# Column sums of the modulation: folded in DRAM by accumulating DMAs instead of GpSimd's partition reduction

## The chip, the cores and the metric

The kernel runs on one core of a Trainium2 chip. The metric is the device time of one execution in microseconds (us). Time before: median 2902.7 us of three runs (2900.84 to 2907.55). All data are float32 in DRAM; TensorE multiplies in a float32 form in which each operand is split in two parts, so that one product takes three matmuls.

## The reference

A two-layer backbone over 512 latent and 256 context tokens, D = 1024. Each layer is FFN, mixer (gated MLP in layer 0, attention in layer 1), FFN. Every sublayer is modulated by two conditioning vectors, `c` for the latent tokens and `c_ctx` for the context tokens:

```python
def modulation(cond, w_mod, b_mod):
    m = jax.nn.silu(cond) @ w_mod + b_mod
    return jnp.split(m[..., None, :], N_MOD, axis=-1)   # N_MOD = 9

def ffn_sublayer(x, shift, scale, gate, w_in, w_out, ln_g, ln_b):
    y = swiglu(modulate(x, shift, scale), w_in, w_out)   # x * (1 + scale) + shift
    return layer_norm(ALPHA * x + 0.5 * gate * y, ln_g, ln_b)
```

For one layer `m` has nine pieces of 1024 numbers: shift, scale and gate for each of the three sublayers. The change touches only how these pieces are summed.

## The kernel before

**Sublayers.** `body` runs six sublayers in order: FFN, gated MLP and FFN of layer 0 (called 0, 1 and 2 here), then FFN, attention and a latent-only FFN of layer 1 (3, 4, 5). In each, TensorE (PE) runs the input projection, then the output projection, half of the 1024 columns at a time. The weights come as 128x512 blocks of 256 KB by DMAs from the SP queue into six buffers `raw`; ScalarE (ACT) casts each into the high part of `w` and VectorE (DVE) subtracts for the low part (`split_later`; all calls of the helper `Pinned` have line 81). Activations go out to DRAM on GpSimd's queue (`act<-stage`) and come back on SP's (`q<-act`), to be split into `acts`.

**Ends of sublayers.** At the end of an output projection (`end.run`, `closing`) each of the six blocks of 128 rows gets its last products; then DVE adds them to the residual and takes statistics (`add_gated`: `q`, `z`, `st`; `norm_stats`: `mv`, `ve`), GpSimd takes the power -1/2 (`rs`, line 174), DVE makes the bias `nb` (line 670), ACT normalises `z`, PE transposes it (`ps<-ident,z`), and GpSimd's queue stores it (`zhat<-z`, line 1808). `rs` and `nb` are not pinned: a scheduler may place them among the other instructions, while calls through `Pinned` (SP, and `self.pool`) keep the order in which the program issues them. Every engine and queue runs its instructions in order.

**Residual adds.** In the first half of the output projections of sublayers 1, 2 and 3, DVE also applies the gain and bias of the LayerNorm to the residual (`z<-z,zraw`, `residual`). In these stretches, around 1020 to 1100, 1565 to 1645 and 2085 to 2170 us, DVE has nearly as much to do per slot as PE.

**Modulation as filler.** 16 of the 18 pieces are made while the sublayers run (`MOD_PLAN` says which in which). `fill` is called about once per slot; it runs what has become due in `pending` (`later(n, f)` runs f after n more fills), then one step of `mod_unit`. For a unit (l, i), and for each half of its 1024 columns, there is one accumulator `acc` of 128x512 for each conditioning vector: two for the units before (1,5), one for the rest. In each of eight steps DVE adds a 128x512 block of `w_mod` times a column of the condition to them (`acc<-mraw,cs,acc`). Then the 128 rows of `acc` must be added up. Before, GpSimd does it in place (`partition_all_reduce`, line 370, 56 times), and a DMA of 2 KB adds row 0 (line 371) onto the bias that a DMA has put in the DRAM tile `mod` [2, 1024].

**Use of the sums.** Units with i % 3 == 2 are gates: `load_gate` reads a row by a broadcasting DMA, 128x1024, before an output projection. Of each pair of the others (shift, scale), `mod_columns`, READ_LATER = 4 fills after both are sent, reads the rows by DMAs on SP's queue (`s<-mod`, four or two, 8x128); `finish`, 3 fills later, turns them by one small PE transpose and copies them into `modT`, which the next input projection reads.

**Start of the second part of the gated MLP (sublayer 1).** The gated half `v` is spilled to DRAM on GpSimd's queue (`v_spill<-q`), six chunks of six blocks. After the last chunk its statistics give `rs` 128x6 on GpSimd, SP loads the first pieces back (`v<-v_spill`), ACT and DVE normalise them (`vn`), and PE multiplies them with the spatial weights (`ps<-w_sT,vn`). Ahead of that, PE has two projections (`ps<-h,w`) to do.

Of the kernel before, what the change touches and what calls it, by code (L numbers as in the profile page):

```python
# [1 line left out]

# [4 lines left out]

F32 = mybir.dt.float32
F32R = mybir.dt.float32r
AF = mybir.ActivationFunctionType  # L10
ALU = mybir.AluOpType
AX = mybir.AxisListType

P = 128
D = 1024
KD = D // P
# [26 lines left out]
ZRAW_BUFS = 3  # L43

READ_LATER, TURN_LATER = 4, 7

FIRST_OPEN = [(2, 0), (3, 0), (4, 0)]
SECOND_OPEN = [(2, 1), (0, 0), (3, 1), (1, 0), (4, 1), (0, 1), (5, 0), (1, 1), (5, 1)]
# [7 lines left out]
CLOSE, CLOSE_LAT = 6, 8  # L56
# [29 lines left out]
class Backbone:  # L86
# [260 lines left out]

    def mod_unit(self, l, i):

        nc, io = self.nc, self.io  # L350
        nconds = self.nconds(l, i)
        m = self.mods[l, i] = self.dram.tile([2, D], F32, name=f"mod{l}{i}")
        for c in range(nconds):
            self.pool.dma_start(m[c : c + 1, :], io["b_mod"][l, i * D : i * D + D].unsqueeze(0))
        for half in range(2):
            accs = [self.acc() for _ in range(nconds)]
            for k in range(KD):
                raw, dve = self.next_raw(), self.dve
                for c in range(nconds):
                    cs = self.cs[:, c * KD + k : c * KD + k + 1]  # L360
                    if k:
                        dve.scalar_tensor_tensor(accs[c], raw, cs, accs[c], ALU.mult, ALU.add)
                    else:
                        dve.tensor_scalar(accs[c], raw, cs, None, ALU.mult)
                self.filler_raw()
                if k < KD - 1:
                    yield
            s = slice(half * 512, half * 512 + 512)
            for c in range(nconds):
                nc.gpsimd.partition_all_reduce(accs[c], accs[c], P, bass_isa.ReduceOp.add)  # L370
                nc.gpsimd.dma_start(m[c : c + 1, s], accs[c][0:1, :], accum_op=ALU.add)
            yield
        self.mod_sent.add((l, i))
        if i % 3 == 2:
            self.mod_done.add((l, i))
        elif {(l, i - i % 3), (l, i - i % 3 + 1)} <= self.mod_sent:
            self.later(READ_LATER, lambda: self.mod_columns(l, i - i % 3))

    def nconds(self, l, i):
        return 2 if (l, i) < (1, 5) else 1  # L380
# [1 line left out]
    def mod_columns(self, l, i):  # L382

        n = self.nconds(l, i)
        srcs = [self.mods[l, x][c : c + 1, :] for c in range(n) for x in (i, i + 1)]
        view = self.modT[l][:, 0:n, i * KD : (i + 2) * KD]
        f = self.columns(view, [s.rearrange("o d -> (o d)") for s in srcs])
        assert TURN_LATER > READ_LATER

        def finish():  # L390
            f()
            self.mod_done.update({(l, i), (l, i + 1)})

        self.later(TURN_LATER - READ_LATER, finish)
# [101 lines left out]
    def load_gate(self, l, i, nblocks):  # L496
        self.need((l, i))
        gate = self.main.tile([P, 2, D], F32, tag="gate", bufs=1, name="gate")
        for c in range(2 if nblocks > NB_LAT else 1):
            self.sp.dma_start(gate[:, c], self.mods[l, i][c : c + 1, :].to_broadcast([P, D]))  # L500
        self.gate = gate

    def mod_vectors(self, l, i, nconds, prev):
# [269 lines left out]
    def out_proj_latent(self, acts, l, i, factor, end, prev):  # L773

        n = acts.n
        order = acts.orders(n, KEPT_LAT, READ_BACK_LAT)[0]
        acts.feed(0, 4)
        self.new_z(NB_LAT)
        residual = iter(())
        banks = {}  # L780
        for x in range(n - CLOSE_LAT):
            ws = self.weights(2)
            for b in range(NB_LAT):
                for half in range(2):
                    if not x:
                        banks[b, half] = self.bank()
                    self.products(banks[b, half], b, [acts.of(order[x])], ws[half : half + 1], x == 0, False)
                if b % 2:
                    self.flush()
                    self.pump(1)  # L790
                    if b == 1:
                        acts.prepare(0, x + AHEAD + 1)
                        next(residual, None)
            self.release(2)
            acts.feed(0, 4)
            if x == 1:
                residual = self.residual(prev, NB_LAT)
                next(residual, None)
                self.load_gate(l, i + 2, NB_LAT)
        for _ in residual:  # L800
            pass
        st = self.stats(NB_LAT)
        end.begin(NB_LAT)
        x = n - CLOSE_LAT + AHEAD + 1
        ws = self.weights(CLOSE_LAT)
        rest = order[n - CLOSE_LAT :]
        for b in range(NB_LAT):
            for k in range(0, CLOSE_LAT, 2):
                fs = rest[k : k + 2]
                self.products(banks[b, 0], b, [acts.of(f) for f in fs], ws[k : k + 2], False, k == CLOSE_LAT - 2)  # L810
                if not b:
                    acts.feed(0, 4)
                    for _ in range(2):
                        acts.prepare(0, x)
                        x += 1
                self.flush()
                if b == NB_LAT - 1:
                    self.release(2)
                    self.pump(2)
            self.add_gated(b, 0, banks[b, 0], factor, st[b])  # L820
        self.flush()
        ws = self.weights(CLOSE_LAT)
        self.flush()
        self.pin(False)

        def closing(b):
            self.products(banks[b, 1], b, [acts.of(f) for f in rest], ws, False)
            return [lambda: self.add_gated(b, 1, banks[b, 1], factor, st[b])], st[b]

        end.last(NB_LAT, closing)  # L830
# [1058 lines left out]
```

## Time and profile before

| | |
|---|---|
| median of three runs | 2902.7 us |
| profiled execution | 2903.88 us, span 2902.0 us |
| TensorE busy / mean granted clock | 2801.8 us (97%) / 0.990 |
| VectorE / ScalarE / GpSimd busy | 2112.4 / 1164.8 / 411.0 us |
| partition reductions on GpSimd | 56, 199.0 us in all |
| DMA bytes | 426.84 MB |

A row of the timeline gives start, duration, engine, line, operation, output and inputs, the count of merged instructions, and in brackets the idle time before it with the instruction that ended it. PE is busy nearly all the time, so what matters are the few waits on it, and its clock behind them.

### The profile page before, as it was taken

What the parts mean: (1) busy time and instruction counts of PE and PEld (TensorE: products, weight loads), DVE (VectorE), ACT (ScalarE), POOL (GpSimd) and SP (SyncE); (2) the same over time, 40 slices, a digit from 0 to 9 for tenths busy, and PEclk for the clock granted to TensorE, in tenths of its full rate; (3) what the DMA queues carried; (4) which work ended last, traced back from release to release, by engine and by line L of the source; (5) the groups of instructions that cost most, each with busy time, mean ns of one, the idle gap of its engine ahead of it and who ended that gap; (6) DMA issues with size and microseconds to landing.
All of it is one profiled execution on the core that took longest, in us unless ns stands there. A gap on an engine that the chain in (4) does not pass through costs nothing.

```text
span 2902.0 us, 40507 instructions
## 1 busy us (share of the span) xinstructions
PE 2801.8 (97%) x14454; PEld 2514.5 (87%) x14454; DVE 2112.4 (73%) x3692; ACT 1164.8 (40%) x2232; POOL 411.0 (14%) x379
## 2 busy tenths in 40 slices
PE   7899999999999999999999999999999989999998
PEld 5899988788899977899999788999978778888886
DVE  6888877587777777498787968877785577733445
ACT  6333432532344432453333226333432556632322
POOL 1010112234401112000010210000021121100001
PEclk9999999999999999999999999999999999999999
DMA  7434375355544474344335644433474423444352
GB/s 236 123 115 127 105 241 175 121 197 182 179 153 155 145 243 143 116 148 127 120 119 198 194 127 132 142 117 118 143 242 146 132 83 51 141 141 137 102 167 98
DMA packets 407090, 426.84 MB, mean 147 GB/s; under 512 B 27944, under 2 KB 308584, under 8 KB 406888
## 3 DMA queue, kind: packets, MB, share of 16 engines
q1 hardware_dynamic: 387400, 361.36, 40.4%
q0 software_dynamic: 19488, 62.90, 6.8%
q8 instruction: 113, 1.85, 0.3%
q14 instruction: 89, 0.73, 0.1%
HBM read 362.95 MB, written 63.41 MB: 147 GB/s over the span
## 4 chain that ended last, share of the span: by engine, by line
PE 73%; DVE 9%; DMA 8%; ACT 5%; issue 3%; SPq 1%; POOL 0%; DVEq 0%; ACTq 0%; POOLq 0%
PE ps L81 72%; DMA v<-v_spill 3%; ACT v L1135 2%; DVE acc L81 1%; DVE w L81 1%; DVE w L148 1%; SPq L81 1%; DMA zraw<-in_ln_b_dram 1%; ACT w L147 1%; DMA mraw<-in_w_mod_dram 1%; DMA q<-act 1%; PE pp L81 1%; DVE z L81 1%; DMA raw<-in_w_mod_dram 1%; DVE acts L81 1%
## 5 line engine op out<-in xcount | busy, mean ns | idle before, releaser
L81 PE MATMUL ps<-comb,w 128*128 128x384 f32 x5544 | 977.0, 336 | 23.3 <-DVE comb L81 9.8
L81 PEld LDWEIGHTS ps<-comb,w 128*128 128x128 f32 x5544 | 966.5, 189 | 29.2 <-DVE comb L81 13.3
L81 PE MATMUL ps<-w,acts 128*128 128x512 f32 x3768 | 870.5, 392 | 17.3 <-DVE acts L81 17.0
L81 PEld LDWEIGHTS ps<-w,acts 128*128 128x128 f32 x3768 | 706.7, 189 | 173.1 <-DVE acts L81 26.7
L81 ACT CAST w<-raw 128x512 fp32r<-128x512 f32 x573 | 355.0, 620 | 735.4 <-PE ps L81 673.4
L81 DVE TENSOR_TENSOR w<-raw,w 128x512 fp32r<-128x512 f32 x573 | 422.6, 742 | 244.7 <-ACT w L81 242.4
L81 PE MATMUL ps<-h,w 128*128 128x384 f32 (+2 forms) x2304 | 450.0, 356 | 6.8 <-DVE w L148 3.5
L81 PEld LDWEIGHTS ps<-h,w 128*128 128x128 f32 x2304 | 406.9, 190 | 44.7 <-DVE w L148 3.9
L370 POOL PARTITION_ALL_REDUCE acc<-acc x56 | 199.0, 3561 | 789.0 <-DVE acc L81 610.2
L81 PE MATMUL ps<-w,h 128*128 128x512 f32 x1200 | 278.4, 393 | 5.8 <-DVE kT L142 3.1
L81 PEld LDWEIGHTS ps<-w,h 128*128 128x128 f32 x1200 | 226.4, 190 | 54.8 <-ACT h L580 3.6
L81 DVE TENSOR_TENSOR q<-q,ps 128x384 f32<-128x384 f32 (+1 forms) x282 | 157.1, 557 | 151.6 <-PE ps L81 126.1
L81 DVE SCALAR_TENSOR_TENSOR acc<-mraw,cs,acc 128x512 f32<-128x512 f32 x340 | 250.2, 770 | 4.5 <-DMA mraw<-in_w_mod_dram 4.5
L81 ACT CAST w<-sums 128x512 fp32r<-128x512 f32 x198 | 122.9, 621 | 232.5 <-DVE sums L290 112.2
L81 ACT CAST acts<-q 128x384 fp32r<-128x384 f32 (+1 forms) x262 | 129.7, 520 | 198.9 <-DMA q<-act 159.8
L81 POOL DMA_DIRECT2D act<-stage x84 | 47.1, 561 | 994.2 <-DVE stage L81 803.0
L148 DVE TENSOR_TENSOR w<-raw,w 128x512 fp32r<-128x512 f32 x171 | 118.7, 713 | 75.2 <-ACT w L147 74.6
L81 DVE TENSOR_TENSOR acts<-q,acts 128x384 fp32r<-128x384 f32 (+1 forms) x262 | 138.5, 561 | 9.3 <-ACT acts L81 9.3
L81 DVE TENSOR_TENSOR w<-sums,w 128x512 fp32r<-128x512 f32 x198 | 135.4, 684 | 1.9 <-ACT w L81 1.9
L147 ACT CAST w<-raw 128x512 fp32r<-128x512 f32 x171 | 102.2, 619 | 57.2 <-PE ps L81 34.5
L174 POOL TENSOR_TENSOR rs<-ve,mhalf 128x1 f32<-128x1 f32 (+3 forms) x47 | 42.3, 901 | 495.7 <-DVE ve L171 264.8
L81 DVE TENSOR_TENSOR z<-z,zraw 128x512 f32<-128x512 f32 x88 | 72.9, 828 | 43.3 <-DMA zraw<-in_ln_g_dram 36.5
(193 smaller groups left out, 2119.8 us busy)
## 6 DMA issues: line engine op xcount, KB each, us to landing
raw<-in_ffn_w_in_dram SPq DMA_DIRECT2D x388, 256.0 KB
mraw<-in_w_mod_dram SPq DMA_DIRECT2D x256, 256.0 KB
raw<-in_ffn_w_out_dram SPq DMA_DIRECT2D x176, 256.0 KB
q<-act SPq DMA_DIRECT2D x216, 192.0 KB
act<-stage POOLq DMA_DIRECT2D x74, 384.0 KB, 2.7
raw<-in_gmlp_w_in_dram SPq DMA_DIRECT2D x96, 256.0 KB
zhat<-z POOLq DMA_DIRECT2D x26, 512.0 KB, 3.0
raw<-in_gmlp_w_out_dram SPq DMA_DIRECT2D x48, 256.0 KB
```

Of the source, the lines that this page charges most:

```text
L81: return self.tc.keep_in_program_order(f(*args, **kwargs))
L147: self.act.copy(hi, src)
L148: self.lows.append((key, lambda: self.dve.tensor_tensor(lo, src, hi.bitcast(F32), ALU.subtract)))
L174: self.last_rstd = self.nc.gpsimd.tensor_tensor(rs, ve, self.mhalf[:, 0:1].to_broadcast([P, n]), ALU.pow).ins
L370: nc.gpsimd.partition_all_reduce(accs[c], accs[c], P, bass_isa.ReduceOp.add)
L1135: act.activation(vr[:, b], vr[:, b], AF.Identity, bias=n, scale=r)
```

## The change

The tile `mod` now holds, for each conditioning vector, all 128 rows. `acc` is stored whole by a DMA of 256 KB on GpSimd's queue; the bias is added to row 0 by an accumulating DMA; then accumulating DMAs from DRAM to DRAM add the lower half of the rows to the upper half: 64, 32 and 16 rows for shift and scale, and on to 1 row for gates. Each is issued in a fill of its own, by GpSimd's in-order queue, and waits for the one before it to land. The last 16 rows of shift and scale are read by `mod_columns` as 128x128 tiles (`rows`, SP's queue), turned by PE (18 transposes of 128x128 in all where there were five small ones) and summed by DVE (`tensor_reduce`). `mod_columns` runs one fill after the last fold instead of four after the last sum. The gate of the last sublayer is loaded at x = 10 of `out_proj_latent` instead of x = 1, with a fill in each of the steps before. 56 partition reductions, their 56 DMAs of 2 KB and 28 bias DMAs go; 56 stores, 16 bias DMAs and 72 folds come.

```diff
-        m = self.mods[l, i] = self.dram.tile([2, D], F32, name=f"mod{l}{i}")
-        for c in range(nconds):
-            self.pool.dma_start(m[c : c + 1, :], io["b_mod"][l, i * D : i * D + D].unsqueeze(0))
+        m = self.mods[l, i] = self.dram.tile([nconds, P, D], F32, name=f"mod{l}{i}")
...
             for c in range(nconds):
-                nc.gpsimd.partition_all_reduce(accs[c], accs[c], P, bass_isa.ReduceOp.add)
-                nc.gpsimd.dma_start(m[c : c + 1, s], accs[c][0:1, :], accum_op=ALU.add)
+                self.pool.dma_start(m[c, :, half * 512 : half * 512 + 512], accs[c])
             yield
...
+        def fold(n):
+
+            if n == P:
+                self.pool.dma_start(m[:, 0:1], bias.to_broadcast([nconds, 1, D]), accum_op=ALU.add, max_dma_last_dim=4096)
+            else:
+                self.pool.dma_start(m[:, 0:n], m[:, n : 2 * n], accum_op=ALU.add, max_dma_last_dim=4096)
+            if n > (1 if i % 3 == 2 else PARTIAL):
+                self.later(0, lambda: fold(n // 2))
+                return
...
+                self.later(0, lambda: self.mod_columns(l, i - i % 3))
+
+        self.later(0, lambda: fold(P))
...
-        srcs = [self.mods[l, x][c : c + 1, :] for c in range(n) for x in (i, i + 1)]
...
+        rows = self.sm([4, P], "rows4", 1)
+        for c in range(n):
+            for x in range(2):
+                src = self.mods[l, i + x][c, 0:PARTIAL].rearrange("r (k p) -> (r k) p", p=P)
+                self.sp.dma_start(rows[:, 2 * c + x], src)
 
         def finish():
-            f()
+            ps = self.bank()
+            for x in range(2 * n):
+                self.tp(ps[:, x * P : x * P + P], rows[:, x])
+            for c in range(n):
...
+                self.dve.tensor_reduce(dst, src, AX.X, ALU.add)
...
             if x == 1:
                 residual = self.residual(prev, NB_LAT)
                 next(residual, None)
+            if x < n - CLOSE_LAT - 4:
+                self.fill()
+            elif x == n - CLOSE_LAT - 4:
                 self.load_gate(l, i + 2, NB_LAT)
```

In the changed kernel line 81 has become 83, 174 has become 176, 670 is 688, 1808 is 1829 and 1104 is 1125.

**Where instructions moved, 1: the end of sublayer 2.** GpSimd's order before: `rs` of a block (a power of `ve`), then the store `zhat` of that block, for the six blocks in turn.

```order
L174 TENSOR_TENSOR rs_16078<-ve_16077,mhalf 128x1
L1808 DMA zhat_0_16047<-z 128x1024
L174 TENSOR_TENSOR rs_16110<-ve_16109,mhalf 128x1
L1808 DMA zhat_1_16048<-z 128x1024
L174 TENSOR_TENSOR rs_16164<-ve_16163,mhalf 128x1
L1808 DMA zhat_2_16049<-z 128x1024
L174 TENSOR_TENSOR rs_16218<-ve_16217,mhalf 128x1
L1808 DMA zhat_3_16050<-z 128x1024
```

GpSimd's order in the changed kernel at the same place; `mod_14204` is the gate (1,2), whose folds run on here.

```order
L83 DMA mod_14204<-mod_14204 2x64x1024
L176 TENSOR_TENSOR rs_16089<-ve_16088,mhalf 128x1
L176 TENSOR_TENSOR rs_16121<-ve_16120,mhalf 128x1
L1829 DMA zhat_0_16058<-z 128x1024
L83 DMA mod_14204<-mod_14204 2x32x1024
L1829 DMA zhat_1_16059<-z 128x1024
L176 TENSOR_TENSOR rs_16175<-ve_16174,mhalf 128x1
L176 TENSOR_TENSOR rs_16229<-ve_16228,mhalf 128x1
L83 DMA mod_14204<-mod_14204 2x16x1024
L1829 DMA zhat_2_16060<-z 128x1024
L1829 DMA zhat_3_16061<-z 128x1024
```

The six `rs` come in three pairs, and folds stand between the pairs.

DVE's order before, at the same place (`q`, `z`, `st` and `mv` close one block; `nb` is what its normalisation waits for):

```order
L171 TENSOR_SCALAR ve_16077<-mv 128x1
L670 SCALAR_TENSOR_TENSOR nb<-mv,rs_16078 128x1
L688 SCALAR_TENSOR_TENSOR q<-ps,gate 128x512
L699 TENSOR_TENSOR z<-z,q 128x512
L700 BN_STATS st<-z 128x6
L665 BN_AGGR mv<-st 128x2
L171 TENSOR_SCALAR ve_16109<-mv 128x1
L670 SCALAR_TENSOR_TENSOR nb<-mv,rs_16110 128x1
```

DVE's order in the changed kernel:

```order
L173 TENSOR_SCALAR ve_16088<-mv 128x1
L706 SCALAR_TENSOR_TENSOR q<-ps,gate 128x512
L717 TENSOR_TENSOR z<-z,q 128x512
L718 BN_STATS st<-z 128x6
L683 BN_AGGR mv<-st 128x2
L173 TENSOR_SCALAR ve_16120<-mv 128x1
L688 SCALAR_TENSOR_TENSOR nb<-mv,rs_16089 128x1
L688 SCALAR_TENSOR_TENSOR nb<-mv,rs_16121 128x1
```

The `nb` of the first block now stands behind the closing of the second; the third and fourth, and the fifth and sixth blocks are paired in the same way, and so are those at the end of sublayer 3. The ends of sublayers 0 and 1 keep the order of before.

**Where instructions moved, 2: sublayer 1, where the second part of the gated MLP begins.** GpSimd's order before; ISA on `acc` is the partition reduction, `mod_6499` belongs to unit (0,7) and `mod_6986` to (0,8), `rs` 128x6 are the statistics of `v`.

```order
L1104 DMA v_spill_5516<-q 128x512 x6
L370 ISA acc<-acc 128x512
L371 DMA mod_6499<-acc 16x1x32
L370 ISA acc<-acc 128x512
L371 DMA mod_6499<-acc 16x1x32
L81 DMA mod_6986<-in_b_mod_dram 16x64 x2
L1104 DMA v_spill_5517<-q 128x512 x6
L174 TENSOR_TENSOR rs_7199<-ve_7198,mhalf 128x6
L370 ISA acc<-acc 128x512 x2
```

GpSimd's order in the changed kernel; (0,7) is `mod_6497` here.

```order
L83 DMA mod_6497<-acc 128x512 x2
L1125 DMA v_spill_5519<-q 128x512 x3
L83 DMA mod_6497<-in_b_mod_dram 2x1024
L176 TENSOR_TENSOR rs_7197<-ve_7196,mhalf 128x6
L83 DMA mod_6497<-mod_6497 2x64x1024
L83 DMA mod_6497<-mod_6497 2x32x1024
L83 DMA mod_6497<-mod_6497 2x16x1024
L83 DMA act_0_7146<-stage 128x768
```

The sums of (0,7) were complete before the last spills; now its three folds stand behind `rs`.

SP's order before at that place (`mod_6038` is unit (0,6)):

```order
L81 DMA s_7128<-mod_6038 8x128
L81 DMA s_7128<-mod_6499 8x128
L81 DMA mraw<-in_w_mod_dram 128x512
L81 DMA raw<-in_gmlp_w_in_dram 128x4x128
L81 DMA s_7146<-in_gmlp_w_s_dram 128x128
L81 DMA v<-v_spill_5512 128x6x128 x2
```

SP's order in the changed kernel:

```order
L83 DMA rows_7126<-mod_6034 128x128
L83 DMA rows_7126<-mod_6497 128x128
L83 DMA mraw<-in_w_mod_dram 128x512
L83 DMA raw<-in_gmlp_w_in_dram 128x4x128
L83 DMA s_7144<-in_gmlp_w_s_dram 128x128
L83 DMA v<-v_spill_5514 128x6x128 x2
```

The reads of the sums stand where they stood, ahead of the first pieces of `v`; what they wait for is now the last fold of (0,7). The same order holds for the pair (0,3), (0,4) ahead of the end of sublayer 0, where they stand among the loads of `raw`.

More of the change, by code (lines that the diff above doesn't have):

```diff
@@ L4 @@
 import concourse.tile as tile
-from concourse import bass_isa, mybir
+from concourse import mybir
 from concourse.masks import make_identity
@@ L45 @@
 READ_LATER, TURN_LATER = 4, 7
+PARTIAL = 16
 FIRST_OPEN = [(2, 0), (3, 0), (4, 0)]
@@ L348, in mod_unit @@
     def mod_unit(self, l, i):
-        nc, io = self.nc, self.io
         nconds = self.nconds(l, i)
-        m = self.mods[l, i] = self.dram.tile([2, D], F32, name=f"mod{l}{i}")
-        for c in range(nconds):
-            self.pool.dma_start(m[c : c + 1, :], io["b_mod"][l, i * D : i * D + D].unsqueeze(0))
+        m = self.mods[l, i] = self.dram.tile([nconds, P, D], F32, name=f"mod{l}{i}")
         for half in range(2):
@@ L367, in mod_unit @@
                     yield
-            s = slice(half * 512, half * 512 + 512)
             for c in range(nconds):
-                nc.gpsimd.partition_all_reduce(accs[c], accs[c], P, bass_isa.ReduceOp.add)
-                nc.gpsimd.dma_start(m[c : c + 1, s], accs[c][0:1, :], accum_op=ALU.add)
+                self.pool.dma_start(m[c, :, half * 512 : half * 512 + 512], accs[c])
             yield
[L373 to L377, printed above, removed]
+        bias = self.io["b_mod"][l, i * D : i * D + D].unsqueeze(0).unsqueeze(0)
+        def fold(n):
[6 more added lines that the diff above has]
+                return
+            self.mod_sent.add((l, i))
+            if i % 3 == 2:
+                self.mod_done.add((l, i))
+            elif {(l, i - i % 3), (l, i - i % 3 + 1)} <= self.mod_sent:
+                self.later(0, lambda: self.mod_columns(l, i - i % 3))
+        self.later(0, lambda: fold(P))
     def nconds(self, l, i):
@@ L384, in mod_columns @@
         n = self.nconds(l, i)
-        srcs = [self.mods[l, x][c : c + 1, :] for c in range(n) for x in (i, i + 1)]
-        view = self.modT[l][:, 0:n, i * KD : (i + 2) * KD]
-        f = self.columns(view, [s.rearrange("o d -> (o d)") for s in srcs])
-        assert TURN_LATER > READ_LATER
-        def finish():
-            f()
+        rows = self.sm([4, P], "rows4", 1)
[3 more added lines that the diff above has]
+                self.sp.dma_start(rows[:, 2 * c + x], src)
+        def finish():
+            ps = self.bank()
+            for x in range(2 * n):
+                self.tp(ps[:, x * P : x * P + P], rows[:, x])
+            for c in range(n):
+                src = ps[:, 2 * c * P : 2 * (c + 1) * P].rearrange("p (x r k) -> p x k r", x=2, r=PARTIAL)
+                dst = self.modT[l][:, c, i * KD : (i + 2) * KD].rearrange("p (x k) -> p x k", x=2)
+                self.dve.tensor_reduce(dst, src, AX.X, ALU.add)
             self.mod_done.update({(l, i), (l, i + 1)})
@@ L499, in load_gate @@
         for c in range(2 if nblocks > NB_LAT else 1):
-            self.sp.dma_start(gate[:, c], self.mods[l, i][c : c + 1, :].to_broadcast([P, D]))
+            self.sp.dma_start(gate[:, c], self.mods[l, i][c, 0:1].to_broadcast([P, D]))
         self.gate = gate
```

## The prediction

> **What bounds the kernel now.** I read the page first: the span, the busy times and the chain that ended last.
>
> ```profile
> span 2902.0 us, 40507 instructions
> PE 2801.8 (97%) x14454; PEld 2514.5 (87%) x14454; DVE 2112.4 (73%) x3692; ACT 1164.8 (40%) x2232; POOL 411.0 (14%) x379
> PE 73%; DVE 9%; DMA 8%; ACT 5%; issue 3%; SPq 1%; POOL 0%; DVEq 0%; ACTq 0%; POOLq 0%
> L370 POOL PARTITION_ALL_REDUCE acc<-acc x56 | 199.0, 3561 | 789.0 <-DVE acc L81 610.2
> ```
>
> PE works 97% of the span; only 100.2 us of it are waits. GpSimd, which the change relieves of 199.0 us, has 0% of the chain. So taking its work away gains nothing by itself; a gain can come only through what the reductions do to others, and a loss through each new wait that reaches PE. I therefore looked for the stages where PE waits, in the table of windows. These three hold the residual adds:
>
> ```profile
> 1020.00:1100.00 80.00, 73.18 (x315) 58.14 (x314) 66.95 (x104) 27.03 (x54) 17.99 (x10) 0.98 0.72 238
> 1565.00:1645.00 80.00, 74.78 (x318) 59.64 (x317) 66.03 (x99) 26.93 (x53) 17.88 (x10) 0.98 0.76 247
> 2085.00:2170.00 85.00, 79.31 (x341) 64.02 (x341) 68.59 (x103) 28.06 (x56) 17.38 (x9) 0.98 0.75 243
> ```
>
> After the length come PE, weight loads, DVE, ACT, GpSimd, the granted clock, the DMA share and GB/s. PE is idle for 6.82, 5.22 and 5.69 us, 17.7 in all, and DVE is 81 to 84% busy. The timelines of GpSimd, DVE and PE in the second stretch show why:
>
> ```profile
> 1589.15 3.58 POOL L370 PARTITION_ALL_REDUCE acc<-acc  x1 [78.75 <-ACT acts L81]
> ...
> 1593.59 3.47 POOL L370 PARTITION_ALL_REDUCE acc<-acc  x1
> ...
> 1589.55 2.73 DVE L81 TENSOR_TENSOR w<-raw,w 128x512 fp32r<-128x512 f32 x1
> ...
> 1593.13 3.48 DVE L81 TENSOR_TENSOR z<-z,zraw 128x512 f32<-128x512 f32 x2
> ...
> 1597.65 0.68 DVE L81 TENSOR_TENSOR w<-raw,w 128x512 fp32r<-128x512 f32 x1
> ...
> 1599.19 1.40 DVE L81 TENSOR_TENSOR z<-z,zraw 128x512 f32<-128x512 f32 x2
> ...
> 1626.53 5.76 PE L81 MATMUL ps<-w,acts 128*128 128x512 f32 x18 [2.46 <-DVE acts L81]
> 1632.77 4.40 PE L81 MATMUL ps<-w,acts 128*128 128x512 f32 x18 [0.48 <-DVE acts L81]
> ```
>
> While a reduction runs, a DVE subtraction takes 2.73 us instead of 0.68, and a pair of adds 3.48 instead of 1.40: about 2.05 us lost for each reduction. Each stretch has four, two pairs. PE then waits for DVE's `acts`, and after the 2.46 us wait 18 matmuls take 5.76 us against 4.40: 1.4 us more, the clock being lower for a while.
>
> **The gain.** With the reductions gone, DVE gets back 12 x 2.05 = 24.6 us in the three stretches; that is the upper end. On PE there are 17.7 us of waits and 3 x 1.4 of slow clock to regain, 21.9. I take 20, as some of the waits are short and may have another cause. The lower end is 6: DMAs are at 72 to 76% there, and if transfers set the pace, DVE's gain turns into waits for data. In other stages DVE has room, and the reductions end no wait of PE that I found, except at the start of the gated MLP's second part (below). The other removals (56 DMAs of 2 KB and 28 bias issues) lie on GpSimd, which idles: nothing.
>
> **The cost of a fold.** The profile before has no fold. Its nearest rows, from the list of DMA issues with size and median time to landing, and the row of GpSimd's queue (packets, MB, share of the 16 engines' span):
>
> ```profile
> zsum<-in_ln_b_dram POOLq DMA_DIRECT2D x4, 512.0 KB, 11.2
> zsum<-zraw POOLq DMA_DIRECT2D x8, 256.0 KB, 5.2
> zsum<-q POOLq DMA_DIRECT2D x8, 256.0 KB, 4.0
> mod<-acc POOLq DMA_DIRECT2D x56, 2.0 KB, 3.1
> q0 software_dynamic: 19488, 62.90, 6.8%
> ```
>
> For two conditioning vectors the folds move 512, 256 and 128 KB. The first row is the same size and also DRAM to DRAM: 11.2. The second accumulates 256 KB: 5.2. For 128 KB I take 4.0, between 3.1 and 5.2. A chain of three is then 20.4 us. The short end: 5.2 + 4.0 + 3.1 = 12.3, if the 11.2 is only what four at once cost each other. The long end: the queue moved 62.90 MB in 6.8% of 16 engines' 2902 us, 3157 engine-us, or 19.9 KB per us and engine. The folds' outermost count is two (2x64x1024), that of each row above but the 2 KB one is 128. If a transfer is dealt out by that count, two engines carry it: 524/39.8 = 13.2 us plus some 3.1 fixed, then 6.6 and 3.3 plus as much, 32.4 for the chain. I take 20.4 for the sum and keep both ends.
>
> The Trainium skill, "DMA: Bandwidth & Descriptors", Rules for kernel authors ("Use all 16 engines"), says that an outermost dimension of c < 16 confines a DMA to at most c engines; by it the chain is the long one. No run here shows it yet.
>
> **Start of the second part of the gated MLP.** GpSimd, SP and PE there:
>
> ```profile
> 780.19 1.75 POOL L174 TENSOR_TENSOR rs<-ve,mhalf 128x6 f32<-128x6 f32 x1 [7.08 <-DVE acc L362]
> ...
> 770.29 1.45 SPq L81 DMA_DIRECT2D s<-mod  x4
> 774.85 0.36 SPq L81 DMA_DIRECT2D mraw<-in_w_mod_dram  x1
> ...
> 776.59 0.96 SPq L81 DMA_DIRECT2D v<-v_spill  x2
> ...
> 788.26 1.59 PE L81 MATMUL ps<-w_sT,vn 128*128 128x256 f32 x12
> ...
> 796.39 10.12 PE L81 MATMUL ps<-h,w 128*128 128x384 f32 x48 [3.27 <-DVE su L1205]
> ```
>
> Before, SP reads the sums at 770.29 and issues the load of `v` at 776.59; PE has its two projections until 788.2 and goes straight on. Now the four reads of `rows` hold SP until the 16-row fold of (0,7) has landed, and that chain begins on GpSimd only behind `rs`, at 780.19 + 1.75 = 782.0. With 20.4 us it ends at 802.4. SP then needs 1.45 us for the reads and 776.59 - 774.85 = 1.7 for the three issues ahead of `v`: 805.6. From the load's issue to PE took 11.7 us before, of which the last 6.3 came after `rs`; `rs` is ready this time, so I take 9: PE resumes at 814.6. That is 26.4 us later, and 1.4 for the slow clock behind it; against it the wait of 3.27 with its slow clock goes, since the reductions beside it go and DVE has run ahead: 4.7 less. Net 23. Short end (chain 12.3): 15. Long end (32.4): 35. Behind the blocked reads, `raw` and `mraw` wait too, but PE stands still itself, so they add nothing.
>
> **End of sublayers 2 and 3.** GpSimd and PE at the end of sublayer 2, and PE at that of sublayer 3:
>
> ```profile
> 1735.51 0.60 POOL L174 TENSOR_TENSOR rs<-ve,mhalf 128x1 f32<-128x1 f32 x1 [31.39 <-DVE ve L171]
> ...
> 1739.59 0.56 POOL L174 TENSOR_TENSOR rs<-ve,mhalf 128x1 f32<-128x1 f32 x1 [0.97 <-DVE ve L171]
> ...
> 1746.02 0.56 POOL L174 TENSOR_TENSOR rs<-ve,mhalf 128x1 f32<-128x1 f32 x1 [2.26 <-DVE ve L171]
> ...
> 1751.32 1.11 POOL L174 TENSOR_TENSOR rs<-ve,mhalf 128x1 f32<-128x1 f32 x1 [2.28 <-DVE ve L171]
> ...
> 1737.63 1.09 PE L81 MATMUL ps<-ident,z 128*128 128x128 f32 x8 [0.75 <-ACT z L1806]
> 1738.48 4.35 PE L81 MATMUL ps<-w,acts 128*128 128x512 f32 x18
> ...
> 1765.79 3.91 PE L81 MATMUL ps<-comb,w 128*128 128x384 f32 x12 [3.17 <-ACT pieces L81]
> ...
> 2261.59 1.09 PE L81 MATMUL ps<-ident,z 128*128 128x128 f32 x8 [0.75 <-ACT z L1806]
> ```
>
> PE transposes each block as soon as ACT has normalised it, and waits 0.75 us for the first. By the new order on DVE the first block of a pair waits for the second's statistics, which came 4.08 us (1739.59 - 1735.51) and 5.30 us (1751.32 - 1746.02) later. The second block's `ve` comes a little earlier than that, as it no longer waits for a `nb` of its own: I put the first block back by 3.4 us and the third by 4.4. PE has the next 18 matmuls only behind the transposes in its order, so nothing covers this; each wait draws 1.4 of slow clock. That is 10.6. In sublayer 2 a later wait, 3.17 us at 1765.79, is taken up in part (by about 2.5 with its clock): +8. In sublayer 3 nothing as long follows, and the last pair comes a little later too: +12. Short ends 3 each, if PE had slack that I miss; long ends 13 and 16. The folds between the `rs` here have an earlier one to wait for that was issued a slot or two before, so they add nothing by the middle price.
>
> **End of sublayer 0 and the rest.** GpSimd's first reduction of (0,4)'s second half, SP's reads and PE's small transpose:
>
> ```profile
> 511.64 3.66 POOL L370 PARTITION_ALL_REDUCE acc<-acc  x1 [24.41 <-DVE acc L81]
> ...
> 534.95 1.59 SPq L81 DMA_DIRECT2D s<-mod  x4
> ...
> 541.12 0.24 PE L81 MATMUL ps<-ident,s 32*128 32x32 f32 x1
> ```
>
> The first reduction starts when DVE has done `acc`, at about 512; storing them (3.1) and the bias in the next slot put the first fold at 519 to 520. The chain of 20.4 ends at 540, the rows land some 3 us later, and PE wants them at 541.1: +3 (short end 0, long end 15). The other pairs have 10 us more of slack: nothing. The 18 transposes cost PE 18 x 0.85/8 = 1.9 (eight of them take 1738.48 - 1737.63), less the five small ones: +2 with DVE's sums. The moved gate is read long before it is used: nothing.
>
> **Sum.** -20 + 23 + 8 + 12 + 3 + 2 = +28, from the profiled 2903.88 to 2931.9. The median of the runs lies 1.2 lower, so 2930.7, in round numbers 2931.
>
> **Rivals.** (a) Two engines carry a fold. Then the gated MLP loses 35 instead of 23, sublayer 0's end 15 instead of 3, and the reads ahead of sublayer 4 (pair (1,3), (1,4)) hold SP's weight loads for some 6: 2931 + 30 = 2961. For it: the shapes; against it: no row of before shows a large transfer so shaped. The skill's rule named above is this mechanism.
>
> (b) Faster: the folds land as quickly as the 2 KB DMA, 3.1 us each, because the queue has little else to do, and DVE's whole gain reaches PE. The chain in the gated MLP then ends at 791.3, `v` is issued at 794.5, and PE resumes 6.3 to 9 later, near 802: 14 late, less 4.7, and 1.4 more, so +11. The pairs cost their short ends, 3 and 3, and sublayer 0's end nothing; the transposes are hidden in those waits: -24.6 + 11 + 6 = -8, or 2895. It decides if the three folds together stay under some 10 us. Against it: both rows of 256 KB take longer than the 2 KB one.
>
> (c) The reductions only stood beside DMA-bound work in the three stretches: the gain is 6, not 20: 2931 + 14 = 2945. Against it: the four DVE rows above.
>
> (d) Gains and losses cancel: short ends at the gated MLP (15) and 3 at each end, with 20 gained: about 2905.
>
> **Chances.** Forecast, 2915 to 2943: 0.42; (a) 0.28; (c) 0.08; (b) 0.14; (d) 0.08. The predicted time is the forecast's, 2931. The range has to take in (b)'s 2895 at its near side and (a) with its spread, up to 2975: 2892 to 2975. Within 0.2% (5.8 us, about what a measurement of this kernel can tell from no change) lies (d): 0.08; faster is (b), 0.14; slower the rest, 0.78.
>
> **What would show it.** In the changed profile: no DVE subtraction of 2.7 us, and the three stretches with PE idle for under 2 us each; the three folds of (0,7) after `rs`, their landings 11, 5 and 4 us (or 16, 10 and 6: rival a), and PE idle for some 25 us near 790; two waits of about 4 us at each end of sublayers 2 and 3, with 12 or 18 slow matmuls behind each. I am wrong if the wait near 790 is under 10 us, if the pairs cost no wait, or if the stretches keep their waits without the reductions.

## The result and the profile after

The changed kernel takes 3138.9 us (median of four runs, 3135.73 to 3142.59), the kernel before in the same comparison 2904.78: the ratio is 1.0806, 95% interval 1.079 to 1.0821. It is 234 us slower, far outside the range of 2892 to 2975. The page of the profile after, in the lines that answer to those of before (span, busy times, the chain that ended last, and the folds' group):

```profile
span 3137.5 us, 40489 instructions
PE 2834.6 (90%) x14467; PEld 2543.8 (81%) x14467; DVE 2027.8 (65%) x3696; ACT 1167.8 (37%) x2232; POOL 272.9 (9%) x383
PE 59%; DMA 15%; issue 10%; DVE 8%; ACT 5%; SPq 1%; POOL 1%; DVEq 0%; POOLq 0%; ACTq 0%
L83 POOL DMA_DIRECT2D mod<-mod x72 | 73.3, 1018 | 421.0 <-DMA mod<-mod 384.2
```

PE now waits 3137.5 - 2834.6 = 302.9 us, against 100.2 before, and its busy time has grown by 33 us for almost the same matmuls, with a mean granted clock of 0.953 against 0.990: that is the slow clock behind the waits. DMA's share of the chain has gone from 8 to 15%. GpSimd, relieved of its reductions, stands idle for 421.0 us ahead of folds, 384.2 of them because the fold before has not landed. The list of DMA issues gives the median time to landing by size. The folds of 256 and of 128 KB include a few of units with one conditioning vector; the last line, for comparison, is another accumulating DMA of 256 KB, with 128 rows outermost:

```profile
mod<-mod POOLq DMA_DIRECT2D x12, 512.0 KB, 28.2
mod<-mod POOLq DMA_DIRECT2D x16, 256.0 KB, 13.7
mod<-mod POOLq DMA_DIRECT2D x16, 128.0 KB, 8.4
zsum<-zraw POOLq DMA_DIRECT2D x8, 256.0 KB, 4.0
```

By these medians a chain of three takes 50.3 us, not 20.4 (nor the 32.4 of the long end). Where PE waits is in the table of its waits (total, times, longest):

```profile
PE ps L83 <- DMA rows<-mod: 65.1, 5, 22.1
PE ps L83 <- ACT vn L143: 61.8, 2, 57.0
PE ps L83 <- DVE q L83: 24.7, 4, 8.7
PE ps L83 <- DMA s<-in_gmlp_w_s_dram: 24.6, 2, 16.5
PE ps L83 <- ACT z L1827: 18.6, 8, 4.2
PE ps L83 <- DVE acts L83: 13.0, 3, 12.6
```

The largest, at the start of the gated MLP's second part, read along GpSimd, SP and PE:

```profile
847.88 1.46 POOL L83 DMA_DIRECT2D mod<-mod  x1
872.22 1.09 POOL L83 DMA_DIRECT2D mod<-mod  x1 [22.88 <-DMA mod<-mod]
885.87 0.94 POOL L83 DMA_DIRECT2D mod<-mod  x1 [12.56 <-DMA mod<-mod]
...
840.59 54.95 SPq L83 DMA_DIRECT2D rows<-mod  x4
...
897.09 1.01 SPq L83 DMA_DIRECT2D v<-v_spill  x2
...
904.19 0.58 PE L83 MATMUL ps<-w_sT,vn 128*128 128x256 f32 x1 [57.01 <-ACT vn L143]
```

The three folds follow `rs` as the order said, and from the first one's issue to the end of SP's wait pass 47.7 us. SP stands in the reads of `rows` for 54.95 us, only then issues the load of `v`, and PE waits 57.0 us. The same trace also shows a unit with one conditioning vector, (1,5), whose first fold also moves 256 KB, but as 64x1024:

```profile
1673.12 0.80 POOL L83 DMA_DIRECT2D mod<-mod  x1 [1.84 <-DMA mod<-in_b_mod_dram]
1677.50 0.79 POOL L83 DMA_DIRECT2D mod<-mod  x1 [3.58 <-DMA mod<-mod]
1682.15 0.76 POOL L83 DMA_DIRECT2D mod<-mod  x1 [3.87 <-DMA mod<-mod]
```

The next fold can go 4.4 us after it. At 872.22 the fold of 2x32x1024, the same 256 KB, held the next one for 13.7 us. This is the first sign that the shape decides, and not the addition in DRAM. The DMA packets of the same trace show how. While the first fold at the gated MLP runs, GpSimd's queue has this share of the time of the 16 DMA engines (packets, MB, share; window 852 to 871 us):

```profile
q0 software_dynamic: 121, 0.49, 13.1%
```

13.1% of 16 engines is two engines, busy throughout. Taken one by one, the fold has 128 packets of 4 KB, and during 18 of its 21 us exactly two are under way at once; in the fold of 64x1024 above it is about sixteen for most of its 2 us. The 896 packets of 8 bytes that the slow fold has besides are over by 851.4 us, so that they are not what makes it long.

### The profile page after: what moved, and what is told of

It is laid out like the page before. It is cut to its first block, busy times and chain, and to the rows that moved or that the text cites. A ratio compares the mean times of both kernels' runs of the same rounds, so it can differ in the third digit from the quotient of the medians.

```text
span 3137.5 us, 40489 instructions
## 1 busy us (share of the span) xinstructions
PE 2834.6 (90%) x14467; PEld 2543.8 (81%) x14467; DVE 2027.8 (65%) x3696; ACT 1167.8 (37%) x2232; POOL 272.9 (9%) x383
## 4 chain that ended last, share of the span: by engine, by line
PE 59%; DMA 15%; issue 10%; DVE 8%; ACT 5%; SPq 1%; POOL 1%; DVEq 0%; POOLq 0%; ACTq 0%
PE ps L83 58%; DMA mod<-mod 4%; DMA v<-v_spill 4%; DMA raw<-in_ffn_w_in_dram 2%; ACT v L1156 1%; DMA mraw<-in_w_mod_dram 1%; DMA q<-act 1%; SPq L83 1%; DVE acc L83 1%; DVE w L150 1%; DVE w L83 1%; ACT w L149 1%; DVE z L83 1%; DMA mod<-acc 1%; PE pp L83 1%
## 5 line engine op out<-in xcount | busy, mean ns | idle before, releaser
L83 PEld LDWEIGHTS ps<-comb,w 128*128 128x128 f32 x5544 | 972.1, 190 | 50.3 <-DVE comb L83 13.6
L83 PE MATMUL ps<-w,acts 128*128 128x512 f32 x3768 | 882.0, 396 | 28.8 <-DVE acts L83 13.0
L83 PEld LDWEIGHTS ps<-w,acts 128*128 128x128 f32 x3768 | 719.2, 192 | 184.1 <-DVE acts L83 15.3
L83 DVE TENSOR_TENSOR w<-raw,w 128x512 fp32r<-128x512 f32 x573 | 390.8, 687 | 240.8 <-ACT w L83 240.3
L83 DVE SCALAR_TENSOR_TENSOR acc<-mraw,cs,acc 128x512 f32<-128x512 f32 x340 | 241.6, 745 | 62.1 <-DMA mraw<-in_w_mod_dram 62.1
L150 DVE TENSOR_TENSOR w<-raw,w 128x512 fp32r<-128x512 f32 x171 | 114.4, 687 | 82.6 <-ACT w L149 82.1
L1156 ACT ACTIVATE v<-v,v_nb,rs 128x128 f32<-128x128 f32 x138 | 58.3, 484 | 196.1 <-DMA v<-v_spill 196.1
L83 POOL DMA_DIRECT2D mod<-mod x72 | 73.3, 1018 | 421.0 <-DMA mod<-mod 384.2
L83 PE MATMUL ps<-w_sT,vn 128*128 128x256 f32 x288 | 44.9, 307 | 69.1 <-ACT vn L143 61.8
```

The source lines that it names most:

```text
L83: return self.tc.keep_in_program_order(f(*args, **kwargs))
L150: self.lows.append((key, lambda: self.dve.tensor_tensor(lo, src, hi.bitcast(F32), ALU.subtract)))
L1156: act.activation(vr[:, b], vr[:, b], AF.Identity, bias=n, scale=r)
```

## The experiments

**Theory E and its rivals.** E: a fold with an outermost count of two is carried by two engines; the waits for it make the loss. Rival A: accumulating from DRAM to DRAM is slow by itself. The first kernel has this edit, by which the same bytes go in as many DMAs:

```diff
-                self.pool.dma_start(m[:, 0:n], m[:, n : 2 * n], accum_op=ALU.add, max_dma_last_dim=4096)
+                r = m.rearrange("c r d -> r c d")
+                self.pool.dma_start(r[0:n], r[n : 2 * n], accum_op=ALU.add, max_dma_last_dim=4096)
```

> The folds move the same bytes in as many DMAs, but the rows are outermost (64x2x1024 instead of 2x64x1024), and the scheduler now also leaves the rs, nb and z of the ends of sublayers 2 and 3 one after the other, as in the kernel before. Theory E (two engines carry a fold whose outermost count is two): 512 KB lands in some 8 us instead of 28.2, 256 KB in 4 to 5 instead of 13.7, the wait of 57.0 us before the spatial product and those for rows (22.1, 19.8, 15.6) fall under 5 each; the time comes to 2880 to 2920. Rival A (an accumulating DMA from DRAM to DRAM is slow by itself, since it reads its destination too): the folds still take over 20 us for 512 KB, and the time stays above 3080.

Measured: 2887.2 us, ratio 0.9933 to the kernel before (0.9917 to 0.9948). The order of two dimensions turns the change from 234 us slower to 0.7% faster. The folds in its list of DMA issues, and GpSimd's queue while the first fold of (0,7) runs (window 759 to 763 us):

```profile
mod<-mod POOLq DMA_DIRECT2D x12, 512.0 KB, 7.0
mod<-mod POOLq DMA_DIRECT2D x16, 256.0 KB, 5.3
mod<-mod POOLq DMA_DIRECT2D x16, 128.0 KB, 4.0
...
q0 software_dynamic: 144, 0.52, 77.1%
```

The queue now has 77.1% of the 16 engines' time. Rival A falls as the cause of the whole: the addition was kept. In PE's timeline none of the waits for `rows` is left, and the spatial product starts at 787.08.

The second kernel keeps the slow shape and leaves out the addition, so that the rows are not summed:

```diff
-                self.pool.dma_start(m[:, 0:n], m[:, n : 2 * n], accum_op=ALU.add, max_dma_last_dim=4096)
+                self.pool.dma_start(m[:, 0:n], m[:, n : 2 * n], max_dma_last_dim=4096)
```

> The folds copy instead of adding (the rows are not summed), in the shape of the changed kernel, 2x64x1024. Theory E: a plain copy by two engines is slow as well, 512 KB in 13 us or more (262 KB for each engine at the 19.9 KB per us of the queue's row), and most of the loss stays, above 3000 us. Rival A: without the addition 512 KB lands in 5 to 8 us and the time falls to 2880 to 2940.

Measured: one run of 2990.2 us. Its folds:

```profile
mod<-mod POOLq DMA_DIRECT2D x12, 512.0 KB, 16.4
mod<-mod POOLq DMA_DIRECT2D x16, 256.0 KB, 8.4
```

So the copy is slow too, as E has it. As an estimate, with the 3.1 us of a small DMA taken off, 262 KB for each of two engines in 13.3 us is 19.7 KB per us, the rate that the prediction drew from the queue's row (19.9). With the addition it is 262 / 25.1 = 10.4, about half. The packets agree: in the fold of (0,7) one of 4 KB takes 159 ns in the median as a copy and 328 ns with the addition, in the slow shape and with the rows outermost alike. E's forecast of a time above 3000 missed by 10 us. Without the addition the kernel is 149 us faster in this shape; with the rows outermost all of the loss goes although the addition stays.

The third is the kernel before without its reductions, one line less; only row 0 is added, so the sums are left out:

```diff
-                nc.gpsimd.partition_all_reduce(accs[c], accs[c], P, bass_isa.ReduceOp.add)
```

> The kernel before without the reductions over the partitions; row 0 alone is added (the other rows are left out). Nothing else comes. Theory G (the reductions slow DVE, and that costs PE its waits in the three stretches of the residual adds and at the start of the gated MLP's second part): 20 to 26 us less than before, 2877 to 2883. Rival C (the stretches are held by transfers): at most 6 us less, 2896 or more.

Measured: 2876.35 us, ratio 0.9895 (0.9876 to 0.9914). By the spans, 2875.8 against 2902.0, it is 26.2 us less, just over the upper edge of theory G; by the medians of this comparison it is 32.2 less. Rival C falls. The three stretches in this kernel:

```profile
1020.00:1100.00 80.00, 79.48 (x349) 64.97 (x348) 67.65 (x120) 29.13 (x57) 4.20 (x6) 1.00 0.85 276
1565.00:1645.00 80.00, 79.76 (x352) 65.54 (x351) 67.06 (x115) 25.68 (x50) 5.72 (x8) 1.00 0.79 253
2085.00:2170.00 85.00, 85.00 (x376) 70.10 (x375) 68.27 (x121) 27.27 (x51) 4.41 (x6) 1.00 0.74 235
```

PE idles for 0.8 us in them, where it idled for 17.7, and DVE gets through more instructions there (120 against 104 in the first) while it is about as busy as before. The DMA share of 72 to 76% before was no limit: it reaches 85% here in the first stretch.

**One place at a time.** Theory W: what costs is that someone waits in order for a slow fold. Rival Q: slow folds hold up the transfers of others. In the kernel with the rows outermost, single units got the slow shape back:

```diff
-                r = m.rearrange("c r d -> r c d")
-                self.pool.dma_start(r[0:n], r[n : 2 * n], accum_op=ALU.add, max_dma_last_dim=4096)
+                r = m if (l, i) in UNITS else m.rearrange("c r d -> r c d")
+                to, src = (m[:, 0:n], m[:, n : 2 * n]) if r is m else (r[0:n], r[n : 2 * n])
+                self.pool.dma_start(to, src, accum_op=ALU.add, max_dma_last_dim=4096)
```

> The kernel with the rows outermost (2887), but the units (0,6) and (0,7) fold in the changed kernel's form, 2x64x1024. Theory W (what costs is that someone waits in order for a slow fold: SP's queue behind the reads of rows): only the wait at the start of the gated MLP's second part comes back; its three folds take 28.2 + 13.7 + 8.4 = 50 us after about 781, so PE resumes near 840 instead of 790: 45 to 60 us more, 2932 to 2947, and no new wait of over 3 us elsewhere. Rival Q (slow folds load two of the engines on which every load runs, and so slow all loads): the loss spreads over many places, and this one is under 25.

Measured: 2926.5 us, 39 above 2887.2 and so below the 45 to 60 expected; by the spans of the profiled executions (2929.4 and 2883.9) 45.5. PE resumes where it was expected, and there is no other new wait of over 3 us:

```profile
839.60 0.58 PE L83 MATMUL ps<-w_sT,vn 128*128 128x256 f32 x1 [47.42 <-ACT vn L143]
```

Next, with (1,2) alone as UNITS:

> As the kernel with the rows outermost, but the gate (1,2) alone folds in the form 2x64x1024; with it the scheduler again puts the rs and nb of the end of sublayer 2 in pairs. Theory P (the pairing makes PE wait for two blocks' statistics): two waits of 4.0 and 4.2 us before ps<-ident,z in sublayer 2, with slow clock behind them and part of the later wait for pieces taken up, 7 to 11 us more than 2887 in the window of that end. Rival: the blocks are ready in any case, no new wait, under 3 us more.

Measured: 2903.7 us, 16.5 above 2887.2. The 7 to 11 us were forecast for the window of that end, and there they came: from the last matmul ahead of the first transposes to the end of the wait for `pieces`, PE takes 39.7 us, against 29.4 with the rows outermost, 10.4 more. GpSimd and PE at the end of sublayer 2:

```profile
1733.98 1.13 POOL L83 DMA_DIRECT2D mod<-mod  x1 [1.14 <-issue]
1734.72 1.55 POOL L1831 DMA_DIRECT2D zhat<-z  x2
1747.76 1.05 POOL L83 DMA_DIRECT2D mod<-mod  x1 [11.50 <-DMA mod<-mod]
1748.46 1.48 POOL L176 TENSOR_TENSOR rs<-ve,mhalf 128x1 f32<-128x1 f32 x2
...
1655.17 45.12 PE L83 MATMUL ps<-w,acts 128*128 128x512 f32 x189 [6.42 <-DVE q L83]
1733.10 1.09 PE L83 MATMUL ps<-ident,z 128*128 128x128 f32 x8 [3.57 <-ACT z L1829]
1750.94 1.97 PE L83 MATMUL ps<-ident,z 128*128 128x128 f32 x8 [7.66 <-ACT z L1829]
```

The pairs cost two waits, as P says. The second is 7.66 us and not 4.2, because here the third and fourth `rs` stand behind a fold that waited 11.50 us for its predecessor. The rest of the 16.5 arose earlier. There is a wait of 6.42 us at 1655.17, 80 us ahead of that end, which W does not explain. It falls just behind a stretch where the slow first fold of (1,2) runs, no one waits for it, and ACT waits 12.25 us for `q<-act`, a load of SP's queue.

With (0,3) and (0,4) as UNITS:

> As the kernel with the rows outermost, but the units (0,3) and (0,4) alone fold in the form 2x64x1024. Theory W: the waits of PE for rows at the end of sublayer 0 come back, 7.4 and 22.1 us, and with slow clock behind them 28 to 34 us more than 2887: 2915 to 2921. Rival Q: under 10 us there, and waits elsewhere.

Measured: 2914.3 us, 27 above (28 to 34 were expected), with waits of 7.05 and 21.76 us for `rows`. W holds at this place.

**The load without the waits.** To tell W from Q, the changed kernel's folds went to tiles that nobody reads, so that its sums are left out:

```diff
-                self.pool.dma_start(m[:, 0:n], m[:, n : 2 * n], accum_op=ALU.add, max_dma_last_dim=4096)
+                other = self.dram.tile([nconds, P, D], F32, name=f"other{l}{i}_{n}")
+                self.pool.dma_start(other[:, 0:n], self.waste[0:nconds, 0:n], accum_op=ALU.add, max_dma_last_dim=4096)
```

> The changed kernel with folds of the same shapes and bytes (2x64x1024 and so on, accumulating), but from a weight tensor into tiles of their own that nobody reads, so that no fold waits for the one before it and no read waits for a fold (the rows are not summed: this work is left out). Theory W: without the waits the time falls to 2885 to 2920, though the two engines are as loaded as in the changed kernel. Rival Q: the loads stay slow, and the time stays above 3000.

Measured: 3010.1 us. Without the waits the kernel is 3138.9 - 3010.1 = 129 us faster, and W as the whole cause falls. But this run still held the paired order and the reads of `rows`, which wait for the bias, itself a DMA of 2x1024 that is issued behind folds of other units. A cleaner pair followed: the kernel before without reductions, its sums untouched, and beside it the 72 folds as a load, added at the end of `mod_unit`; no instruction names their tiles again.

```diff
+        def load(n):
+            other = self.dram.tile([nconds, P, D], F32, name=f"other{l}{i}_{n}")
+            self.pool.dma_start(other[:, 0:n], self.waste[0:nconds, 0:n], accum_op=ALU.add, max_dma_last_dim=4096)
+            if n > (1 if i % 3 == 2 else 16):
+                self.later(0, lambda: load(n // 2))
+
+        self.later(0, lambda: load(64))
```

> The kernel before without its reductions (only row 0 is added, 2876), and beside it the 72 folds of the changed kernel as a mere load: accumulating DMAs of 2x64x1024 and so on from a weight tensor into tiles that nobody reads; no instruction waits for them. Theory Q (slow folds also hold up other transfers that need the same two engines: stores and small sums behind them in GpSimd's queue, and loads): 30 to 110 us above the next run, with landings of raw, mraw and v_spill over 15 us. Theory W (only waiting in order for a fold costs): under 10 us above it.

> The same load in the form 64x2x1024 and so on, so that only the order of two dimensions differs from the run before. By both theories within 12 us of 2876, and no landing of raw over 11 us.

Measured: 2985.3 us with two outermost, 2877.5 with the rows outermost (ratios to the kernel before 1.0271, 1.025 to 1.0291, and 0.99, 0.988 to 0.9919). The same 72 DMAs with the same bytes cost about 1 us over the kernel without reductions when the rows are outermost, and 108 us more in the slow shape, with no one waiting for them: theory Q holds. Of the run with two outermost, the waits of PE and then of DVE, and the landings of the DMAs of `v_spill` (last line):

```profile
PE ps L81 <- ACT acts L81: 28.1, 8, 5.8
PE ps L81 <- ACT vn L141: 26.5, 2, 14.5
PE ps L81 <- ACT z L1815: 16.6, 5, 4.0
...
DVE acc L81 <- DMA mraw<-in_w_mod_dram: 72.7, 27, 12.0
DVE acc L362 <- DMA mraw<-in_w_mod_dram: 20.8, 6, 16.7
...
DMA to landing us min/median/max: 2.3/6.3/28.4
```

DVE stops in order at the filler's loads for 93.5 us (13.0 in the run beside it; 171.0 in the changed kernel), and what PE needs next, `w` and `acts`, stands behind. Loads of `mraw` come by SP's queue, in which there is no fold: so the folds hold up transfers of another queue too. `v_spill`, in GpSimd's own queue, lands after up to 28.4 us, about as long as a fold, against 5.4 in the run beside it. The traces of this pair hold no landings of SP's loads, so that the forecasts for `raw` and `mraw` stay unchecked here. A part of the 108 us, 16.6 us of waits for `z` against 5.9 in the run beside it, is the paired order, which the scheduler chose again with this shape.

How a fold holds up a load of another queue can be read in the changed kernel's trace, where `mraw` lands after up to 21.2 us (9.2 with the rows outermost). GpSimd issues a slow fold, SP a load of `mraw`, and DVE waits for it:

```profile
1042.37 1.46 POOL L83 DMA_DIRECT2D mod<-mod  x1
1067.93 1.12 POOL L83 DMA_DIRECT2D mod<-mod  x1 [15.12 <-DMA mod<-mod]
...
1048.38 0.50 SPq L83 DMA_DIRECT2D mraw<-in_w_mod_dram  x1
...
1069.56 1.41 DVE L362 SCALAR_TENSOR_TENSOR acc<-mraw,cs,acc 128x512 f32<-128x512 f32 x2 [17.36 <-DMA mraw<-in_w_mod_dram]
```

The load has 128 packets of 2 KB. Of these 112 start between 1049.95 and 1050.96 us; the other 16, as many as two of sixteen engines have of them, start from 1068.29 to 1069.13, when the fold is done.

**Other forms.** Two more kernels change the form of the fold. The first stores half of the accumulator and adds the other half onto it from SBUF, which saves the first fold:

```diff
             for c in range(nconds):
-                self.pool.dma_start(m[c, :, half * 512 : half * 512 + 512], accs[c])
+                self.pool.dma_start(to[c], accs[c][H : 2 * H])
+            self.later(0, lambda to=to, accs=accs: [
+                self.pool.dma_start(t, x[0:H], accum_op=ALU.add) for t, x in zip(to, accs)])
```

> The kernel with the rows outermost (2887), but the accumulators' rows 64 to 127 are stored and rows 0 to 63 added onto them by accumulating DMAs from SBUF, so that the first fold and 7.3 MB of stores go. Theory D (the 11 us by which 2887 stands above the kernel without any sums are transfers: DMAs are at 86 to 91% in the stretches of the residual adds): 3 to 6 us less, 2881 to 2884. Rival: PE waits for none of it, 2885 to 2889.

Measured: 2874.9 us, ratio 0.9892 (0.9877 to 0.9907): the best of all, and level with the kernel that leaves the sums out (0.9895). It lies below the forecasts of D (2881 to 2884) and of its rival alike, so that the 11 us are gone, but not shown to be transfers, as the next run says. That one has a fold for each conditioning vector:

```diff
-                self.pool.dma_start(m[:, 0:n], m[:, n : 2 * n], accum_op=ALU.add, max_dma_last_dim=4096)
+                for c in range(nconds):
+                    self.pool.dma_start(m[c, 0:n], m[c, n : 2 * n], accum_op=ALU.add, max_dma_last_dim=4096)
```

> As the kernel with the rows outermost, but one fold for each conditioning vector, 64x1024 twice, and so on: more DMAs, all with 64, 32 or 16 outermost. Theory E: all engines carry them, so 2880 to 2895, with landings of 4 to 6 us for 256 KB. If it were the number of dimensions and not the outermost count that made the fold slow in the changed kernel, it would be the same too; if it were the two conditions' distance in DRAM, the rows-outermost form would have been slow.

Measured: 2878.0 us, 2 below the forecast, ratio 0.9901 (0.9884 to 0.9917), 256 KB in 5.8 us. It moves as many bytes as the rows-outermost form, and is still 9 us below its 2887.2. These two ran on one chip together, the rows-outermost form on another chip at another time; what separates it from them (0.9933 against 0.9901 and 0.9892) stays open, and D is neither shown nor refuted.

## Why the prediction was wrong

The direction was right. The forecast of 2931 failed at **the cost of a fold**, "I take 20.4 for the sum": the chain took 50.3 us by the medians, 47.7 at the gated MLP. The mechanism was that of rival (a), two engines carry a fold; turning two dimensions round removed the loss. To that rival the prediction gave 0.28 and 2961, and this price failed too, in two terms.

- **The rate.** I took 19.9 KB per us and engine. A plain copy has it (19.7), an accumulating one has half (10.4), so that the long end of 32.4 became 50. "The Trainium skill, DMA: Bandwidth & Descriptors, Rules for kernel authors" says that an outermost dimension of c < 16 confines a DMA to at most c engines, here two. The trace agrees: two packets under way at a time, and 28.2 us against 7.0 for 512 KB. The halving by the addition is this case's measurement.
- **The others' transfers.** I priced only the waits for folds. A load on two engines with nobody waiting costs 108 us. Nothing in the prediction had this term. A load dealt to all engines is complete only when its shares on those two are, as the 16 late packets of `mraw` show.

Together: of the 252 us between 3138.9 and 2887.2, 129 go with the waits in order for folds (3138.9 - 3010.1). The other 123 are the slow transfers and the paired order; the pair of load runs has 108 for the same two. The split is rough, since without the waits several folds are under way together (in that run those of 256 and 128 KB land after 28.4 and 28.5 us too).

Step by step:

- **The gain.** -20 was close: 26.2 by span in the kernel without reductions, with waits and slow clock gone from the stretches; it was the upper end of 24.6 that came nearest.
- **The start of the gated MLP.** +23 (long end 35) became a wait of 57.0 us in the changed kernel. The chain of events was right link by link: folds behind `rs`, SP held by the reads, then `v`. With its units alone slow, PE resumed at 839.6, where 840 had been worked out from the measured landings. The 16.5 us ahead of it, for `s<-in_gmlp_w_s_dram`, are of the other kind: that load was issued at 798.14, while a slow fold ran, and PE could go on at 816.39.
- **Ends of sublayers 2 and 3.** The paired order does cost PE two waits at each; in the changed kernel at sublayer 2, with the later wait for `pieces` shortened from 3.17 to 2.01 as foreseen:

```profile
1907.61 1.35 PE L83 MATMUL ps<-ident,z 128*128 128x128 f32 x8 [4.01 <-ACT z L1827]
1923.58 1.97 PE L83 MATMUL ps<-ident,z 128*128 128x128 f32 x8 [4.19 <-ACT z L1827]
1942.41 3.91 PE L83 MATMUL ps<-comb,w 128*128 128x384 f32 x12 [2.01 <-ACT pieces L83]
```

  The forecast had 3.4 and 4.4. But the order was no cost of its own: with the rows outermost the scheduler put `rs`, `nb` and `z` back one after the other. It came with the fold's shape, in every kernel here where the folds near those ends have the slow one; by what rule the scheduler chooses stays open.
- **End of sublayer 0.** +3 (long end 15) became waits of 7.36 and 22.06 us; "the other pairs have 10 us more of slack: nothing" failed with the same price: `rows` were waited for 15.6 us in sublayer 1 and 19.8 in sublayer 3, where rival (a) had put some 6.
- **Transposes and the moved gate.** Nothing in the runs speaks against +2 and 0; they were not tried apart.
- **Rivals.** (c) fell with the kernel without reductions. (b), a faster kernel, is what the right shape gives, though by another way: its folds take 16.3 us, not under 10, but lie ahead of `rs` and under PE's work. (d) needed the short end of 15 at the gated MLP, where PE waited 57.0 us.

## What to carry to other kernels

Read the outermost count of a DMA's shape before its bytes: a DRAM tile with a small leading dimension, here [2, 128, 1024], made a transfer that fits the bandwidth on paper run on two engines. Price such a transfer not only by who waits for it: here other transfers with a share on those engines landed late, and an in-order engine that stops for one of them holds all that is behind it. To tell the two apart, give the load a destination that nobody reads, once in each shape.

## What the runs showed of the hardware

An accumulating DMA between DRAM tiles of the shape 2x64x1024 had two packets of 4 KB under way at a time and ran at half the rate of a copy of that shape: 28.2 us against 16.4 for 512 KB, with 328 ns for a packet against 159. With the rows outermost, 512 KB took 7.0 us in the median, although a packet still took 328 ns, and the addition cost the kernel next to nothing (72 such DMAs as mere load: 2877.5 against 2876.35 without). While a slow fold ran, 16 of the 128 packets of a load from another queue started 17 us after the others.
